# Sixteen bytes behind each half of a weight buffer: a Trainium2 decoder kernel whose weight tiles get six different start addresses modulo 128

## The chip, the cores and the metric

The kernel runs on one core of a Trainium2 chip. The time is device microseconds of one execution on that core. Engines are named as in the profile: PE is TensorE's matmul, PEld its weight load (of which each matmul has one of its own), DVE VectorE, ACT ScalarE, POOL GpSimd, and SP the engine that issues most DMAs.

## The reference, cut to what matters

Two decoder layers over 512 tokens of width 1024, in float32. Each layer has a half-step SwiGLU, a token mixer (retention in the first layer, forgetting attention in the second), a second half-step SwiGLU and a gated per-layer input ("PLE").

```
def swiglu(x, w_in, w_out):
    g, u = jnp.split(x @ w_in, 2, axis=-1)
    return (jax.nn.silu(g) * u) @ w_out

for i in range(2):
    h = h + 0.5 * swiglu(rmsnorm(h, nw[0]), ffn_w_in[i, 0], ffn_w_out[i, 0])
    h = h + (retention if i == 0 else forgetting_attention)(rmsnorm(h, nw[1]), ...)
    h = h + 0.5 * swiglu(rmsnorm(h, nw[2]), ffn_w_in[i, 1], ffn_w_out[i, 1])
    gate = sigmoid(rmsnorm(h, nw[3]) @ ple_w_gate[i])
    h = h + gate * (p[i] @ ple_w_proj[i])
return rmsnorm(h, final_norm_w)
```

d_model is 1024, d_ff 2816. All weights together are some 200 MB.

## The kernel before

Activations lie transposed: feature blocks of 128 partitions, tokens along the free axis. Each float32 operand is split into a high part, rounded to the fp32r format, and a low part (the rest, in fp32r too), and a product is three matmuls: high weight by high activation, high by low, low by high. `mm3` (L312 to L314) does this for the projections, mostly over 512 tokens at once, with the weight as the stationary operand. `v_part` (L678 to L680) has the weight as the moving operand. The input half of each SwiGLU uses a seven-product scheme on 256-token halves: `product` (L493) does twelve matmuls of 256 columns, four pairs with the high half of a weight tile and then four with the low half. Of the seven products of one block of w_in, two have the stored weights as stationary operand (tile `w`, read in `one` and `three`) and five have sums of weights (tiles `s`) or the remaining quarter (tile `a`); that is 24 matmuls of 84 with `w`. The first two blocks of each SwiGLU are done without the scheme by `plain` (L524), with `w` tiles and again 256 columns.

A weight tile goes through `Weights`. `load` (L75) issues a DMA into a raw buffer on SP. `split` (L82, L83) has ACT write the high half and DVE or POOL the low half. `negated` (L120 to L122) has ACT write the high half and the negated raw weight, and a DMA on POOL's queue adds the weight from memory onto the latter, which leaves the negative of the low half. Either way the tile `w` is one row of 2 x 1024 floats on each partition: the high half, then the low half 4096 bytes behind it.

PE's instructions stand in the order in which the code is written (`manual_schedule`); weights are fetched two tiles ahead of their use (`LOOKAHEAD = 2`, three wide buffers taken in turn). In the last PLE stage, which works on two halves of 256 tokens so that its weights are used twice, five of its wide tiles come from a pool `wkept` of their own.

Pools lie behind each other in SBUF in the order in which they are opened: const, hpool, ua, ub, uc, ud, wraw, wpool, tmp, stat, and behind these the pool of the stage that runs. The start addresses of the built program, in bytes from the start of a partition and modulo 128, are:

| tiles | before: start | start mod 128 of each half |
|---|---|---|
| unit_a, unit_b, unit_c, unit_d (activations), tmp, wraw, hall | 17952 to 177696 | 32 |
| `w`, the three wide buffers of wpool | 140832, 149024, 157216 | 32 and 32 |
| `s` and `a` of the SwiGLU pools | 192224 to 220896 | 96 and 96 |
| `w`, the five kept buffers of the last PLE stage | 184032 to 216800 | 96 and 96 |

A slice of 128 weights is 512 bytes and half of the tokens is 1024 bytes, so every operand slice of PE starts at its tile's value modulo 128.

Of the kernel before, what the change touches and what calls it, by code (L numbers as in the profile page):

```python
# [11 lines left out]
F32 = mybir.dt.float32  # L12
F32R = mybir.dt.float32r
# [4 lines left out]
P = 128  # L18
# [36 lines left out]
class Weights:  # L55
# [17 lines left out]
    def load(self, src):  # L73
        raw = self.raw_pool.tile([P, 1024], F32, name="wraw")
        self.nc.sync.dma_start(out=raw[:, : src.shape[1]], in_=src)  # L75
        return raw

    def split(self, raw, hi, lo, src=None):
        if self.low is None and src is not None:
            self.negated(raw, hi, lo, src)  # L80
            return
        self.nc.scalar.copy(hi, raw)  # L82
        self.low.tensor_tensor(out=lo, in0=raw, in1=hi.bitcast(F32), op=ALU.subtract)  # L83

    def chunk(self, src):
        n = src.shape[1]
        raw = self.load(src)
        if self.spare:
            tiles = [self.spare.pop(0)() for _ in range(4)]
            for i in range(2):  # L90
                self.split(raw[:, 512 * i : 512 * (i + 1)], tiles[i], tiles[2 + i])
            return Halves(tiles[0:2]), Halves(tiles[2:4])
        t = self.pool.tile([P, 2, 1024], F32R, name="w8")
        self.split(raw[:, :n], t[:, 0, :n], t[:, 1, :n], src)
        return t[:, 0, :], t[:, 1, :]

    def emit_parts(self, parts):

        nc = self.nc
        halves = lambda ap: ap.rearrange("p (h c) -> p h c", h=2)  # L100
        tiles = [
            (
                self.raw_pool.tile([P, 1024], F32, name="wraw"),
                self.pool.tile([P, 2, 1024], F32R, name="w8"),
            )
            for _ in range(2)
        ]
        for j0, j1 in parts:
            cs = slice(j0 * P, j1 * P)
            for src, (raw, t) in zip(self.plan, tiles):  # L110
                r, hi, lo = (halves(x)[:, :, cs] for x in (raw, t[:, 0, :], t[:, 1, :]))
                nc.sync.dma_start(out=r, in_=halves(src)[:, :, cs])
                nc.vector.tensor_copy(hi, r)
                nc.vector.tensor_tensor(out=lo, in0=r, in1=hi.bitcast(F32), op=ALU.subtract)
            yield
        self.ready += [(t[:, 0, :], t[:, 1, :]) for _, t in tiles]
# [7 lines left out]
    def first(self, pair):  # L124

        pair.raw = self.load(pair.q)
        pair.t = self.pool.tile([P, 2, 1024], F32R, name="w8")
        hi, lo = pair.t[:, 0, :], pair.t[:, 1, :]
        if pair.direct:
            self.split(pair.raw, hi, lo)  # L130
        else:
            self.negated(pair.raw, hi, lo, pair.q)
# [55 lines left out]
def trunk(ctx, tc, a):  # L188
    nc = tc.nc
# [6 lines left out]
    uc = ctx.enter_context(tc.tile_pool(name="uc", bufs=4))  # L196
    ud = ctx.enter_context(tc.tile_pool(name="ud", bufs=16))
    wraw = ctx.enter_context(tc.tile_pool(name="wraw", bufs=4))
    wpool = ctx.enter_context(tc.tile_pool(name="wpool", bufs=LOOKAHEAD + 1))
    tmp = ctx.enter_context(tc.tile_pool(name="tmp", bufs=7))  # L200
    stat = ctx.enter_context(tc.tile_pool(name="stat", bufs=1))
# [109 lines left out]
    def mm3(out, wh, wl, xh, xl, first, last):  # L311
        nc.tensor.matmul(out, wh, xh, start=first, stop=False)  # L312
        nc.tensor.matmul(out, wh, xl, start=False, stop=False)  # L313
        nc.tensor.matmul(out, wl, xh, start=False, stop=last)  # L314

    def halved(acc):
        hi, lo = temp(F32R), temp(F32R)
        split(acc, hi, lo)
        return hi, lo
# [13 lines left out]
    class Norm:  # L333
# [9 lines left out]
        def halves(self, b):  # L343
            if self.forms is not None:
                return self.quarters(b)
            hi, lo = self.unit(), self.unit()
            split(h[b], hi, lo, self.gain[:, b : b + 1])
            self.hi.append(hi)
            self.lo.append(lo)

        def plain(self, b):

            g = self.gain[:, b : b + 1]
            if b % 2:
                hi, lo = self.unit(), self.unit()
                split(h[b], hi, lo, g)
                both = [(hi[:, c], lo[:, c]) for c in HALVES]
            else:
                both = []
                for i, c in enumerate(HALVES):  # L360
                    u = self.unit() if i == 0 else unit(ud)
                    both.append(tuple(u[:, d] for d in HALVES))
                    split(h[b][:, c], *both[i], g)
            n = 1 + b % 2
            if n == 1:
                self.forms.append({})
            self.forms[b // 2].update({f"b{n}1": both[0], f"b{n}2": both[1]})
# [824 lines left out]
    norms[2].extra = ud  # L1192
    first = W.emit_parts(((0, 1), (1, 2), (2, 4)))
    next(first)
    load_x(1, 2)
    load_x(2, 4)
# [132 lines left out]
```

## Time and profile before

| | |
|---|---|
| time, median of 3 runs | 2228.97 us (2226.98 to 2231.87) |
| span of the profiled execution | 2230.5 us |
| PE busy | 2154.5 us, 97% of the span |
| PEld busy | 1937.5 us |
| DVE, ACT, POOL busy | 1447.1, 1212.3, 450.7 us |
| matmuls | 13525 |
| mean granted TensorE clock | 0.987 |
| DMA | 272 MB, 122 GB/s on the mean |

The profiled execution's own time is not listed apart from its span. The span is above the two faster of the three times, so if it is one of the three, it is the 2231.87 us one, with 1.4 us around the span.

How to read it: a row of the timeline gives start, length, engine, line and operation, `out<-in` by tile names, and the number of instructions merged. The length of a matmul is modelled from start to the end of its pipeline, and successive matmuls overlap; the distance between the starts of successive matmuls, here called the spacing, is what PE's time is made of. For a merged row the spacing is the distance to the start of the next row divided by the count.

### The profile page before, as it was taken

Reading aid. Unit: us, or ns where it says so; the run is one execution under the profiler, and the core shown is the slowest. Engines: PE = TensorE matmul, PEld = TensorE weight load, DVE = VectorE, ACT = ScalarE, POOL = GpSimd, SP = SyncE. Lnnn points to the kernel's source line nnn. Section 1 sums busy time; section 2 is a strip of 40 time slices with the busy share of each in tenths; the row PEclk is TensorE's granted clock in tenths of the full one; section 3 lists DMA queues with packets and bytes.
Section 4 is the critical chain, followed back from the end, with each engine's and each line's share of the span. In section 5 each row is a group of like instructions: output and inputs, shape, how many; then the busy total and the mean of one; then the engine's idle time right before and its main releaser. Section 6 shows DMA issues by size and latency. Waiting matters only on the chain.

```text
span 2230.5 us, 34455 instructions
## 1 busy us (share of the span) xinstructions
PE 2154.5 (97%) x13525; PEld 1937.5 (87%) x13525; DVE 1447.1 (65%) x2631; ACT 1212.3 (54%) x2037; POOL 450.7 (20%) x352
## 2 busy tenths in 40 slices
PE   7999999999999999999997999999999999999998
PEld 7999997888888798989876989898788888999987
DVE  8686776352542776767746677675675686777764
ACT  7565553433233663735555646364786775555543
POOL 0010003444444010101110001012334200110154
PEclk9999999999999999999998999999999999999999
DMA  5465563232222254746464457373622244655631
GB/s 176 113 163 150 138 161 95 81 99 76 88 83 76 85 137 119 170 133 152 129 151 117 114 136 182 113 167 103 153 91 87 69 116 112 159 158 137 152 104 39
DMA packets 86755, 272.33 MB, mean 122 GB/s; under 512 B 9520, under 2 KB 13104, under 8 KB 86592
## 3 DMA queue, kind: packets, MB, share of 16 engines
q1 hardware_dynamic: 63328, 209.78, 28.7%
q0 software_dynamic: 22032, 59.25, 15.9%
q8 instruction: 106, 1.74, 0.3%
q10 hardware_dynamic: 1232, 1.09, 0.1%
q14 instruction: 57, 0.47, 0.1%
HBM read 267.96 MB, written 2.13 MB: 121 GB/s over the span
## 4 chain that ended last, share of the span: by engine, by line
PE 80%; DVE 7%; ACT 6%; DMA 4%; issue 3%; POOL 0%; SPq 0%; DVEq 0%; ACTq 0%; POOLq 0%
PE bank L493 29%; PE bank L314 14%; PE bank L312 13%; PE bank L313 13%; PE bank L524 3%; DMA wraw<-in_ffn_w_in 3%; PE bank L678 2%; PE bank L679 2%; PE bank L680 2%; DVE w L83 1%; DMA w<-in_ple_gate 1%; DVE sums L151 1%; ACT p L982 1%; ACT w L82 1%; DVE tlo L303 1%
## 5 line engine op out<-in xcount | busy, mean ns | idle before, releaser
L82 ACT CAST w<-wraw 128x1024 fp32r<-128x1024 f32 (+1 forms) x232 | 235.1, 1021 | 431.0 <-PE bank L314 252.6
L314 PE MATMUL bank<-unit_a,w 128*128 128x512 f32 x736 | 288.9, 393 | 12.7 <-DMA w<-in_ple_gate 8.4
L312 PE MATMUL bank<-unit_a,w 128*128 128x512 f32 x736 | 289.8, 394 | 1.9 <-ACT w L82 1.6
L313 PE MATMUL bank<-unit_a,w 128*128 128x512 f32 x736 | 287.9, 391 | 0.2 <-DVE unit_a L303 0.2
L82 ACT CAST s<-sums 128x512 fp32r<-128x512 f32 x320 | 191.2, 617 | 155.3 <-DVE sums L151 106.6
L314 PE MATMUL bank<-unit_d,w 128*128 128x512 f32 (+1 forms) x712 | 268.1, 377 | 4.6 <-DVE w L83 4.6
L312 PE MATMUL bank<-unit_d,w 128*128 128x512 f32 (+1 forms) x712 | 269.2, 378 | 3.2 <-ACT w L82 1.6
L313 PE MATMUL bank<-unit_d,w 128*128 128x512 f32 (+1 forms) x712 | 268.3, 377 | 1.8 <-DVE unit_d L303 1.8
L83 DVE TENSOR_TENSOR s<-sums,s 128x512 fp32r<-128x512 f32 x320 | 213.7, 686 | 81.4 <-ACT s L82 80.4
L83 POOL TENSOR_TENSOR w<-wraw,w 128x1024 fp32r<-128x1024 f32 x83 | 202.6, 2445 | 233.5 <-ACT w L82 223.4
L122 POOL DMA_DIRECT2D a<-in_ffn_w_in x80 | 70.1, 876 | 651.4 <-ACT a L121 444.8
L83 DVE TENSOR_TENSOR w<-wraw,w 128x1024 fp32r<-128x1024 f32 (+1 forms) x149 | 175.8, 1185 | 28.3 <-ACT w L82 27.7
L493 PE MATMUL bank<-unit_b,s 128*128 128x256 f32 x880 | 185.9, 278 | 0.0
L493 PE MATMUL bank<-unit_d,s 128*128 128x256 f32 x1140 | 179.2, 277 | 0.0
L314 PEld LDWEIGHTS bank<-unit_a,w 128*128 128x128 f32 x736 | 138.8, 189 | 45.5 <-DMA w<-in_ple_gate 10.1
L493 PE MATMUL bank<-unit_a,s 128*128 128x256 f32 x1260 | 176.1, 277 | 1.9 <-ACT unit_a L376 1.1
L585 DVE SCALAR_TENSOR_TENSOR tmp<-bank,rows 128x512 f32<-128x512 f32 x96 | 66.0, 689 | 165.3 <-PE bank L314 164.0
L312 PEld LDWEIGHTS bank<-unit_a,w 128*128 128x128 f32 x736 | 139.0, 189 | 32.4 <-ACT w L82 3.5
L313 PEld LDWEIGHTS bank<-unit_a,w 128*128 128x128 f32 x736 | 139.0, 189 | 28.8 <-DVE unit_a L303 0.5
L493 PEld LDWEIGHTS bank<-unit_a,s 128*128 128x128 f32 x1260 | 158.8, 188 | 2.7 <-ACT unit_a L376 1.6
L314 PEld LDWEIGHTS bank<-unit_d,w 128*128 128x128 f32 x712 | 134.4, 189 | 30.5 <-DVE w L83 6.6
L312 PEld LDWEIGHTS bank<-unit_d,w 128*128 128x128 f32 x712 | 134.5, 189 | 30.3 <-ACT w L82 3.3
(270 smaller groups left out, 4801.1 us busy)
## 6 DMA issues: line engine op xcount, KB each, us to landing
wraw<-in_ffn_w_in SPq DMA_DIRECT2D x174, 512.0 KB, 4.3
wraw<-in_ffn_w_out SPq DMA_DIRECT2D x64, 512.0 KB, 4.7
w<-in_ffn_w_in POOLq DMA_DIRECT2D x58, 512.0 KB, 5.5
a<-in_ffn_w_in POOLq DMA_DIRECT2D x80, 256.0 KB, 6.2
wraw<-in_ffn_w_out SPq DMA_DIRECT2D x32, 384.0 KB, 3.7
wraw<-in_ret_qk SPq DMA_DIRECT2D x16, 512.0 KB, 3.5
wraw<-in_ret_v SPq DMA_DIRECT2D x16, 512.0 KB, 3.6
wraw<-in_ret_g SPq DMA_DIRECT2D x16, 512.0 KB, 3.5
```

What stands on the lines that cost most here:

```text
L82: self.nc.scalar.copy(hi, raw)
L83: self.low.tensor_tensor(out=lo, in0=raw, in1=hi.bitcast(F32), op=ALU.subtract)
L122: self.nc.gpsimd.dma_start(out=lo, in_=src, accum_op=ALU.add)
L312: nc.tensor.matmul(out, wh, xh, start=first, stop=False)
L313: nc.tensor.matmul(out, wh, xl, start=False, stop=False)
L314: nc.tensor.matmul(out, wl, xh, start=False, stop=last)
L493: add = lambda w, x, start, stop: nc.tensor.matmul(out, w, x, start=start, stop=stop, skip_group_check=True)
L524: nc.tensor.matmul(o[:, HALVES[t]], x[:, ks], y, start=k == t == q == 0, stop=k == KB - 1 and q == 2, skip_group_check=True,)
L585: nc.vector.scalar_tensor_tensor(out=t1, in0=o, scalar=-0.5, in1=n.r, op0=ALU.mult, op1=ALU.mult)
L678: nc.tensor.matmul(os[t], xh, wh[:, js], start=k == 0, stop=False)
L679: nc.tensor.matmul(os[t], xh, wl[:, js], start=False, stop=False)
L680: nc.tensor.matmul(os[t], xl, wh[:, js], start=False, stop=k == KB - 1)
```

## The change

Behind each half of a wide weight tile 16 bytes are left free, and a buffer of 32 bytes is put ahead of the pool, so that each half starts elsewhere modulo 128. The pools behind move by 32 + 3 x 32 = 128 bytes and keep their places modulo 128.

```diff
+    def wide(self):
+        return self.pool.tile([P, 2, 1028], F32R, name="w8")[:, :, 0:1024]
+
...
-        t = self.pool.tile([P, 2, 1024], F32R, name="w8")
+        t = self.wide()
...
-                self.pool.tile([P, 2, 1024], F32R, name="w8"),
+                self.wide(),
...
-        pair.t = self.pool.tile([P, 2, 1024], F32R, name="w8")
+        pair.t = self.wide()
...
     wraw = ctx.enter_context(tc.tile_pool(name="wraw", bufs=4))
+    nc.gpsimd.memset(ctx.enter_context(tc.tile_pool(name="gap0", bufs=1)).tile([P, 8], F32, name="gap0"), 0.0)
     wpool = ctx.enter_context(tc.tile_pool(name="wpool", bufs=LOOKAHEAD + 1))
```

| wide buffer, after | high half mod 128 | low half mod 128 |
|---|---|---|
| 140864 | 64 | 80 |
| 149088 | 96 | 112 |
| 157312 | 0 | 16 |
| the five kept ones | 96, 0, 32, 64, 96 | 112, 16, 48, 80, 112 |

No instruction moves: on every engine the order, the operand shapes and the waits are those of before, but for one added memset of 8 floats per partition, which stands as POOL's first instruction of the program body, ahead of the identity matrix.

## The prediction, made before the changed kernel ran

> **What bounds the kernel now.** I read the page first: the busy shares, then the chain that ended last.
>
> ```profile
> span 2230.5 us, 34455 instructions
> PE 2154.5 (97%) x13525; PEld 1937.5 (87%) x13525; DVE 1447.1 (65%) x2631; ACT 1212.3 (54%) x2037; POOL 450.7 (20%) x352
> PE 80%; DVE 7%; ACT 6%; DMA 4%; issue 3%; POOL 0%; SPq 0%; DVEq 0%; ACTq 0%; POOLq 0%
> ```
>
> PE carries 80% of the chain, and nothing else more than 7%. So the change is worth what it does to the spacing of matmuls. Next I read PE's timeline inside the first SwiGLU, where tiles `w`, `s` and `a` alternate while activations and columns stay alike.
>
> ```profile
> 302.13 1.60 PE L493 MATMUL bank<-unit_a,w 128*128 128x256 f32 x12
> 303.57 0.73 PE L493 MATMUL bank<-unit_b,s 128*128 128x256 f32 x5
> 304.13 0.50 PE L493 MATMUL bank<-unit_c,s 128*128 128x256 f32 x3
> 304.48 0.50 PE L493 MATMUL bank<-unit_b,s 128*128 128x256 f32 x3
> 304.81 0.28 PE L493 MATMUL bank<-unit_c,s 128*128 128x256 f32 x1
> 304.93 1.30 PE L493 MATMUL bank<-unit_a,s 128*128 128x256 f32 x10
> ```
>
> Twelve matmuls on `w` take 303.57 - 302.13 = 1.44 us, 120 ns each; twelve on `s` take 304.93 - 303.57 = 1.36 us, 113.3 ns each. Same form, same activations, 6.7 ns apart. The instructions of the line by tile, and one piece of the chain in order of time, say that this is the rule:
>
> ```profile
> L493 PEld LDWEIGHTS bank<-unit_a,s x1260: 186/188/330, 40.2 to 1081.3; 128*128 128x128 f32 x180
> L493 PEld LDWEIGHTS bank<-unit_a,w x540: 187/192/337, 55.9 to 1078.6; 128*128 128x128 f32 x180
> 127.02 77.44 PE bank L493 x672
> ```
>
> The median weight load is 192 ns from `w` and 188 ns from `s`, so the load is what lengthens. The piece holds eight blocks of 84: 8 x (24 x 120 + 60 x 113.3) = 77.4 us, the row exactly. By the address table, `w` starts at 32 modulo 128, as the activations do, and `s` and `a` at 96. Tile kind and address go together there; the last PLE stage separates them, where `w` tiles at 32 are followed by kept `w` tiles at 96, under the same line and activations.
>
> ```profile
> 2201.69 0.28 PE L312 MATMUL bank<-unit_c,w 128*128 128x256 f32 x1
> ...
> 2202.41 0.28 PE L312 MATMUL bank<-unit_d,w 128*128 128x256 f32 x1
> ...
> 2204.00 0.28 PE L314 MATMUL bank<-unit_d,w 128*128 128x256 f32 x1
> ...
> 2209.78 0.28 PE L312 MATMUL bank<-unit_d,w 128*128 128x256 f32 x1
> ...
> 2212.02 0.28 PE L313 MATMUL bank<-unit_d,w 128*128 128x256 f32 x1
> ```
>
> From 2201.69 to 2202.41, on tiles at 32, six spacings are 0.72 us: 120 ns. From 2202.41 to 2204.00, on a tile at 96, fourteen are 1.59 us: 113.6 ns. So the address matters, not the kind of tile. But from 2209.78 to 2212.02, on other kept tiles at 96, nineteen are 2.24 us: 117.9 ns. The address is not all; how the load falls against the running matmul matters too, and one pair of addresses can hold either spacing for long.
>
> **The change, part by part.** *Matmuls of 256 columns on `w`.* Their counts:
>
> ```profile
> L493 PE MATMUL bank<-unit_b,w 128*128 128x256 f32 x720 | 133.3, 285 | 11.4 <-ACT tmp L545 11.4
> L493 PE MATMUL bank<-unit_d,w 128*128 128x256 f32 x540 | 91.2, 286 | 0.0
> L493 PE MATMUL bank<-unit_a,w 128*128 128x256 f32 x540 | 82.1, 288 | 5.5 <-ACT tmp L545 5.5
> L493 PE MATMUL bank<-unit_c,w 128*128 128x256 f32 x120 | 27.8, 286 | 0.0
> L524 PE MATMUL bank<-unit_b,w x244: 276/283/580, 5.6 to 1825.6; 128*128 128x256 f32 x122
> L524 PE MATMUL bank<-unit_d,w x240: 278/283/415, 6.9 to 1829.9; 128*128 128x256 f32 x120
> L524 PE MATMUL bank<-unit_a,w x168: 279/283/283, 780.8 to 1829.2; 128*128 128x256 f32 x168
> L524 PE MATMUL bank<-unit_c,w x116: 279/283/384, 15.9 to 1827.0; 128*128 128x256 f32 x116
> ```
>
> L493 has 720 + 540 + 540 + 120 = 1920, L524 has 768; L524's median of 283 ns is that of L493's `w`, against 276 for `s`, so the same 120 ns is taken for it. All 2688 at 113.3 would save 2688 x 6.7 ns = 18.0 us: the upper end. The activations stay at 32. A third of the loads come from the buffer at 96 and 112, and two thirds of those from its high half: 597 loads at the pair (32, 96), which the trace shows at 113.3 in the SwiGLUs, 4.0 us. The other 2091 go to 64, 80, 112, 0 and 16, which no row shows; their gain lies between 13.9 us (as at 96) and nothing (as at 32), and below nothing too, since a load could become slower still: no row excludes it, and another 6.7 ns, the one step seen, would cost 13.9 us. The middle of the two spacings seen is nearest to the 117.9 ns row, so I take half, 7.0 us. Together -11.0 us. In PE's cover nothing stands in the way: in the stretch below, one SwiGLU with its norms, PE works 342 of 352 us and DVE, the next, 250.
>
> ```profile
> 43.00:395.00 352.00, 342.01 (x2303) 314.13 (x2304) 250.50 (x402) 186.31 (x303) 49.01 (x43) 0.99 0.51 135
> ```
>
> *Kept tiles of the last PLE stage.* Now at 96 with 113 to 118 ns; afterwards two of five high halves are at 96 again, one each at 0, 32 and 64. Some 200 matmuls by at most 6.7 ns either way: 1.3 us. I take nothing.
>
> *Matmuls of 512 columns.* These are the larger mass.
>
> ```profile
> L312 PE MATMUL bank<-unit_a,w 128*128 128x512 f32 x736 | 289.8, 394 | 1.9 <-ACT w L82 1.6 <-DVE tmp L1016 0.3
> L312 PE MATMUL bank<-unit_d,w 128*128 128x512 f32 x616 | 241.7, 392 | 3.2 <-ACT w L82 1.6 <-DVE unit_b L306 0.6 <-ACT unit_d L302 0.5
> 229.63 0.39 PE L314 MATMUL bank<-unit_d,w 128*128 128x512 f32 x1
> ...
> 231.90 0.39 PE L312 MATMUL bank<-unit_d,w 128*128 128x512 f32 x1
> 384.83 0.40 PE L314 MATMUL bank<-unit_a,w 128*128 128x512 f32 x1
> ...
> 386.91 0.39 PE L314 MATMUL bank<-unit_a,w 128*128 128x512 f32 x1
> ```
>
> From 229.63 to 231.90 ten spacings are 227 ns each, twice the 113.3. So at (32, 32) a long matmul already has its best spacing: the load has double the time, and its slowing is covered. This cover depends on the load ending early, which 4 to 7 ns cannot undo. I cost them at nothing. But between 384.83 and 386.91 nine spacings are 231.1 ns, in a stretch that had not settled. With three lines of 736 + 616, 4056 matmuls have `w` as stationary operand; if other addresses keep them unsettled, 4056 x 4.1 ns = 16.6 us are lost. A gain isn't excluded either: one step of 6.7 ns would be 27 us.
>
> *Writers of `w`.* ACT, DVE, POOL and the adding DMAs now write at other starts, the low halves at odd multiples of 16.
>
> ```profile
> w<-in_ffn_w_in POOLq DMA_DIRECT2D x58, 512.0 KB, 5.5
> w<-in_ple_gate POOLq DMA_DIRECT2D x7, 512.0 KB, 7.3
> PEld bank L314 <- DMA w<-in_ple_gate: 10.1, 4, 4.0
> PE bank L524 <- DMA w<-in_ffn_w_in: 9.3, 1, 9.3
> PEld bank L314 <- DVE w L83: 10.9, 9, 2.2
> L82 ACT CAST w<-wraw 128x1024 fp32r<-128x1024 f32 x200 | 208.7, 1050 | 360.0 <-PE bank L314 181.6 <-issue 96.1 <-PE bank L680 29.3
> L82 ACT CAST s<-sums 128x512 fp32r<-128x512 f32 x320 | 191.2, 617 | 155.3 <-DVE sums L151 106.6 <-PE bank L493 47.8
> ```
>
> Casting into `w` at 32 takes 1050 ns for 1024 elements, into `s` at 96 617 ns for 512: (1050 - 617) / 512 = 0.85 ns per element with 184 ns fixed, no trace of the address. PE waits for these writers 30 us in all in the three waits above; if starts at 16 made each writer a tenth slower, 3 us would be lost there; if faster, 3 us won. I take +1. The added memset of 8 floats stands ahead of 24 us in which POOL has nothing urgent: nothing. If its cover were gone, it would cost less than the 0.9 us of a DMA issue on that engine.
>
> **Sum.** -11.0 + 1 = -10 us against the profiled execution's 2230.5 us span, so 2220.5; against the median of 2229.0 the same -10 gives 2219.
>
> [...] The rows say 113.3 ns beside 120 ns under one line, and the faster when only the tile's address differs. [...]
>
> **The rivals.** *Nothing comes of it:* the other five starts hold 117.9 to 120 ns, only the 4.0 us at (32, 96) come, and writers or the kept tiles take it back: 2225 to 2233. For it: the kept tiles at 96 ran at 117.9 most of the time, and after each change of tile the load must find its place anew. Against: `s` and `a`, five sevenths of the SwiGLU's matmuls, hold 113.3 throughout. *The long matmuls lose their spacing:* with six starts instead of one, each change of tile, and of half, shifts the load against the matmul, and the 512-column matmuls run at 231.1 instead of 227 ns. The place is the output halves of the SwiGLUs, the mixers' projections and the gates. At the full price +16.6 - 10 = +6.6, 2236; without the gain on short ones 2246. It decides once 10 / 0.0041 = 2440 of the 4056 are unsettled. For it: 384.83 to 386.91. Against: at the pair (32, 96) short matmuls hold 113.3, half of 227. *The long ones gain a step too:* 2229 - 10 - 27 = 2192; nothing in the trace shows a spacing so short for long.
>
> **How the numbers follow.** Short matmuls gain and long ones stay: 0.50, own range 2211 (all 18 us) to 2224.5. Nothing: 0.24, 2224.5 to 2233.5. Long ones lose: 0.21, 2233.5 to 2246. Long ones gain: 0.05, below 2211. Two tenths of a per cent, 4.5 us, is about what a measurement of this kernel can tell from no change. Faster is 0.50 + 0.05 = 0.55, same 0.24, slower 0.21. The range 2208 to 2240 leaves out most of the last case and the dearer half of the third.
>
> **What would show it.** Right: the median load from `w` under `product` falls from 192 towards 188 ns, the stretch of 672 matmuls takes less than 77.4 us (76.2 if all gain), and rows of 512 columns stay 227 ns apart. Wrong: `w` rows still 120 apart; 512-column rows at 230 or more over whole stages; or the three waits for writers of `w` grow past 35 us. The prediction falls if spacing follows how the load is started rather than where it reads.

## The result, and the profile after

The changed kernel takes 2248.11 us (median of four runs, 2247.68 to 2248.78) against 2228.15 us for the kernel before (2226.98 to 2231.87): a ratio of 1.0083, with an interval of 1.0067 to 1.0099. The medians stand 20.0 us apart, a quotient of 1.0090, which lies inside that interval. A time of 2219 us and a range up to 2240 were forecast. The profiled execution took 2248.34 us with a span of 2246.5 us, 16.0 us more than the span before. Of all executions behind this document one, of the kernel pad256 below, took 2825.91 us at a granted clock of 0.713, and it is left out of every figure. Line numbers after are three or four higher: `product` is L497, `mm3` L316 to L318, `plain` L528.

The page's span, its busy shares and the chain that ended last:

```profile
span 2246.5 us, 34456 instructions
PE 2174.4 (97%) x13525; PEld 1937.3 (86%) x13525; DVE 1448.5 (64%) x2631; ACT 1213.6 (54%) x2037; POOL 451.1 (20%) x353
PE 83%; DVE 6%; ACT 5%; DMA 3%; issue 2%; POOL 0%; SPq 0%; DVEq 0%; ACTq 0%; POOLq 0%
```

Only PE's row grew by much, 19.9 us; the other engines are within 1.5 us of before, and PE now has 83% of the chain instead of 80%. So the time went into matmuls. Which ones, the timeline of PE says. The longest run of 512-column matmuls in which nothing waits has 244 of them, 243 spacings, from the last part of the first SwiGLU's output into the mixer. Its first and last row, in the kernel before:

```profile
322.85 0.40 PE L312 MATMUL bank<-unit_d,w 128*128 128x512 f32 x1
...
377.95 0.49 PE L312 MATMUL bank<-unit_a,w 128*128 128x512 f32 x1
```

and in the kernel after:

```profile
324.64 0.40 PE L316 MATMUL bank<-unit_d,w 128*128 128x512 f32 x1
...
380.98 0.46 PE L316 MATMUL bank<-unit_a,w 128*128 128x512 f32 x1
```

Before, 55.10 us, 226.7 ns a spacing; after, 56.34 us, 231.9 ns. This stretch, read the same way in every kernel below, is the measure of the long matmuls. The group of the line that showed 289.8 us and a mean of 394 ns before tells the same for the whole program:

```profile
L316 PE MATMUL bank<-unit_a,w 128*128 128x512 f32 x736 | 294.1, 400 | 1.8 <-ACT w L85 1.5
```

The short matmuls, by the chain's pieces in order of time (start, length, what):

```profile
126.57 77.87 PE bank L497 x672
...
1928.82 77.99 PE bank L497 x672
```

The piece of 672 was 77.44 us before and is not shorter but longer. Two places of PE's timeline inside a SwiGLU show why:

```profile
150.12 1.59 PE L497 MATMUL bank<-unit_a,w 128*128 128x256 f32 x12
151.55 0.73 PE L497 MATMUL bank<-unit_b,s 128*128 128x256 f32 x5
...
321.81 1.58 PE L497 MATMUL bank<-unit_a,s 128*128 128x256 f32 x12
323.22 0.75 PE L497 MATMUL bank<-unit_b,a 128*128 128x256 f32 x5
```

Twelve matmuls on `w` still take 1.43 us here, 119 ns each, and twelve on `s`, 113.3 ns each before, take 1.41 us, 117.5 ns each. The sums' buffers kept their starts modulo 128, but here their matmuls run at the slower of the two spacings that the forecast had seen on the kept tiles, 113.6 and 117.9 ns.

To see the whole, I took the distance from each row of PE's timeline to the next and put it to the form of the earlier one; distances over 270 ns (512 columns) or 135 ns (256 columns) for each matmul, and those up to a row that waited, are the rest.

| PE's time, us (count, mean) | before | after | difference |
|---|---|---|---|
| 512 columns | 1056.7 (4652, 227.2 ns) | 1079.6 (4656, 231.9 ns) | +22.9 |
| 256 columns on `w` | 344.5 (2871, 120.0 ns) | 339.4 (2866, 118.4 ns) | -5.1 |
| 256 columns on `s` and `a` | 533.4 (4702, 113.4 ns) | 542.0 (4713, 115.0 ns) | +8.6 |
| rest: waits, a lower clock, other forms | 286.2 | 275.8 | -10.4 |
| first to last matmul | 2220.8 | 2236.8 | +16.0 |

The long matmuls lost 22.9 us; the short ones won 5.1 us on `w` and lost more, 8.6 us, on `s` and `a`. In the rest, PE's waits for ACT's `tmp` in `product` fell from 16.9 to 12.5 us, and the mean granted clock of this execution was 0.989 against 0.987, an estimated 4 us (0.013 of the span before, less 0.011 of the span after); neither was tried by itself. The span of 2230.5 us before belongs to an execution about as long as the slowest of the four timed, so 16 us between the two traces and 20 us between the medians are no contradiction.

### The profile page after: what moved, and what is told of

Same layout as the page of the kernel before. It is cut to its first block, busy times and chain, and to the rows that moved or that the text cites. A ratio compares the mean times of both kernels' runs of the same rounds, so it can differ in the third digit from the quotient of the medians.

```text
span 2246.5 us, 34456 instructions
## 1 busy us (share of the span) xinstructions
PE 2174.4 (97%) x13525; PEld 1937.3 (86%) x13525; DVE 1448.5 (64%) x2631; ACT 1213.6 (54%) x2037; POOL 451.1 (20%) x353
## 4 chain that ended last, share of the span: by engine, by line
PE 83%; DVE 6%; ACT 5%; DMA 3%; issue 2%; POOL 0%; SPq 0%; DVEq 0%; ACTq 0%; POOLq 0%
PE bank L497 32%; PE bank L318 14%; PE bank L316 14%; PE bank L317 14%; PE bank L528 3%; PE bank L683 2%; PE bank L682 2%; PE bank L684 2%; DMA wraw<-in_ffn_w_in 1%; DMA w<-in_ple_gate 1%; DVE w L86 1%; ACT p L986 1%; ACT w L85 1%; ACT p L988 1%; DVE tlo L307 1%
## 5 line engine op out<-in xcount | busy, mean ns | idle before, releaser
L318 PE MATMUL bank<-unit_a,w 128*128 128x512 f32 x736 | 292.3, 397 | 12.9 <-DMA w<-in_ple_gate 8.5
L316 PE MATMUL bank<-unit_a,w 128*128 128x512 f32 x736 | 294.1, 400 | 1.8 <-ACT w L85 1.5
L317 PE MATMUL bank<-unit_a,w 128*128 128x512 f32 x736 | 291.1, 396 | 0.2 <-DVE unit_a L307 0.2
L316 PE MATMUL bank<-unit_d,w 128*128 128x512 f32 (+1 forms) x712 | 271.7, 382 | 3.3 <-ACT w L85 1.5
L318 PE MATMUL bank<-unit_d,w 128*128 128x512 f32 (+1 forms) x712 | 269.8, 379 | 4.7 <-DVE w L86 4.7
L497 PE MATMUL bank<-unit_b,s 128*128 128x256 f32 x880 | 187.9, 280 | 0.0
L318 PEld LDWEIGHTS bank<-unit_a,w 128*128 128x128 f32 x736 | 139.5, 190 | 49.4 <-DMA w<-in_ple_gate 9.9
L497 PE MATMUL bank<-unit_d,s 128*128 128x256 f32 x1140 | 181.1, 279 | 0.0
L497 PE MATMUL bank<-unit_a,s 128*128 128x256 f32 x1260 | 177.3, 278 | 1.9 <-ACT unit_a L380 1.1
L316 PEld LDWEIGHTS bank<-unit_a,w 128*128 128x128 f32 x736 | 139.3, 189 | 35.3 <-ACT w L85 3.5
L318 PEld LDWEIGHTS bank<-unit_d,w 128*128 128x128 f32 x712 | 133.9, 188 | 34.0 <-DVE w L86 6.6
L497 PEld LDWEIGHTS bank<-unit_a,s 128*128 128x128 f32 x1260 | 159.7, 188 | 2.7 <-ACT unit_a L380 1.6
L316 PEld LDWEIGHTS bank<-unit_d,w 128*128 128x128 f32 x712 | 133.5, 188 | 32.4 <-ACT w L85 3.3
```

What stands on the lines that cost most here:

```text
L497: add = lambda w, x, start, stop: nc.tensor.matmul(out, w, x, start=start, stop=stop, skip_group_check=True)
```

## The experiments

All starts below are differences: start of the weight tile minus start of the activations, modulo 256; that 256 is the period came out only on the way (long matmuls are 232.4 ns apart with 128 bytes more, in plus128, and 226.8 with multiples of 256 more, in pad256). The tables ahead of the prediction are modulo 128. By them `s` and `a` stand 64 bytes from the activations before and after; modulo 256 they stand at 192 before and at 64 after, since the pools behind moved by 128 bytes. A number such as 96, 48 or 224 in a kernel's name is a start with the activations at 32, so that it means a difference of 64, 16 or 192. The diffs are against the changed kernel where nothing else is said; `...` marks lines left out. In all of these kernels the five kept buffers of the last PLE stage have no padding; the two lines that see to this, in which `first_pool` is the pool of the three wide buffers, are shown once, in all96.

Each ratio is against runs of the kernel before that were timed together with it: their median is 2231.57 us for the first four experiments, 2229.39 us for the next four and 2230.55 us for the last three.

| kernel | long on `w` (three buffers) | short on `w` | `s`, `a` | 244-row stretch, us (ns a spacing) | ratio, interval |
|---|---|---|---|---|---|
| before | 0 | 0 | 192 | 55.10 (226.7) | 1 |
| after | 32+48, 64+80, 96+112 | the same | 64 | 56.34 (231.9) | 1.0083, 1.0067 to 1.0099 |
| all96 | 64 | 64 | 64 | 56.69 (233.3) | 1.0105, 1.0087 to 1.0124 |
| halves_differ | 0+16, 128+144, 0+16 | the same | 64 | 56.29 (231.6) | 1.0077, 1.0057 to 1.0097 |
| buffers_differ | 32, 64, 96 | the same | 64 | 56.68 (233.3) | 1.0105, 1.0084 to 1.0127 |
| all48 | 16, 144, 16 | the same | 64 | 56.70 (233.3) | 1.0085, 1.0065 to 1.0105 |
| plus128 | 128 | 128 | 64 | 56.47 (232.4) | 1.0088, 1.0058 to 1.0119 |
| both96 | 0 | 0 | 192 | 55.11 (226.8) | 0.9994, 0.9977 to 1.0010 |
| short96 | 0, 128, 0 | 64, 192, 64 | 64 | 55.94 (230.2) | 0.9997, 0.9981 to 1.0013 |
| long96 | 64, 192, 64 | 0, 128, 0 | 64 | 56.49 (232.5) | 1.0126, 1.0101 to 1.0151 |
| short96_256 | 0 | 64 | 192 | 55.11 (226.8) | 0.9959, 0.9941 to 0.9976 |
| short224_256 | 0 | 192 | 192 | 55.14 (226.9) | 1.0045, 1.0031 to 1.0059 |
| pad256 | 0 | 0 | 192 | 55.11 (226.8) | 1.0006, 0.9992 to 1.0020 |

Where one cell has two numbers they are the high and the low half.

### What of the six addresses does the harm?

Three theories. U: the starts are not uniform, so the load must find its place anew at each change of tile or half; one start for all would do no harm wherever it lies. P: the place itself, apart from that of the activations. M: the odd multiples of 16 at which the low halves begin.

**all96: one start for all, 64 bytes on.**

```diff
-        return self.pool.tile([P, 2, 1028], F32R, name="w8")[:, :, 0:1024]
+        if self.pool is not self.first_pool:
+            return self.pool.tile([P, 2, 1024], F32R, name="w8")
+        t = self.pool.tile([P, 2048], F32R, name="w8")[:, 0 : 2048]
+        return t.rearrange("p (a c) -> p a c", a=2)[:, :, 0:1024]
...
-    nc.gpsimd.memset(ctx.enter_context(tc.tile_pool(name="gap0", bufs=1)).tile([P, 8], F32, name="gap0"), 0.0)
+    nc.gpsimd.memset(ctx.enter_context(tc.tile_pool(name="gap0", bufs=1)).tile([P, 16], F32, name="gap0"), 0.0)
     wpool = ctx.enter_context(tc.tile_pool(name="wpool", bufs=LOOKAHEAD + 1))
+    nc.gpsimd.memset(ctx.enter_context(tc.tile_pool(name="gap1", bufs=1)).tile([P, 16], F32, name="gap1"), 0.0)
```

> Wide weight pool moved by 64 bytes, nothing between the halves, and a second gap of 64 bytes behind it, so that every weight half starts at 96 modulo 128 and all that lies behind keeps its place. Theory U (uniformity: the spacing of matmuls settles only where successive weight loads start at the same value modulo 128, and the changed kernel alternates): 512-column matmuls at 227 ns as before, 256-column ones on w tiles at 113 instead of 120, about 2228 - 17 = 2211 us. Theory P (place: each start has a spacing of its own against activations at 32, and 32 was the best for the long ones): 512-column matmuls at about 230.6 ns as the loads at 96 show in the changed kernel, +15 us on them and -17 on the short ones, 2222 to 2232 us. Theory M (odd multiples of 16 are what is slow): as U.

Measured 2253.53 us, 1.0105: no better than the change. The stretch of 244, in PE's timeline:

```profile
324.57 0.39 PE L320 MATMUL bank<-unit_d,w 128*128 128x512 f32 x1
...
381.26 0.45 PE L320 MATMUL bank<-unit_a,w 128*128 128x512 f32 x1
```

56.69 us, 233.3 ns a spacing, and steadily so: with one start for all buffers and halves, and an even one, the long matmuls are worse than with six. U and M fall. P survives only in kind: it had 230.6 ns and 2222 to 2232 us here, and the loss is larger. The same kernel shows something else in its chain:

```profile
126.99 79.15 PE bank L501 x672
...
894.48 76.17 PE bank L501 x672
```

Here `w`, `s` and `a` all stand at 64, so all 672 matmuls are alike in their starts; in the first SwiGLU they take 117.8 ns each, in the second 113.3. One pair of addresses holds either spacing, for a whole stage.

**halves_differ: 16 bytes behind the high half only, buffers 8320 bytes apart.**

```diff
-        return self.pool.tile([P, 2, 1028], F32R, name="w8")[:, :, 0:1024]
...
+        t = self.pool.tile([P, 2080], F32R, name="w8")[:, 0 : 2056]
+        return t.rearrange("p (a c) -> p a c", a=2)[:, :, 0:1024]
...
-    nc.gpsimd.memset(ctx.enter_context(tc.tile_pool(name="gap0", bufs=1)).tile([P, 8], F32, name="gap0"), 0.0)
```

> 16 bytes between the halves, but buffers a multiple of 128 bytes apart: in all three buffers the high half starts at 32 and the low half at 48. U: successive loads alternate inside every group of three, the long matmuls don't settle, 231 to 234 ns, 2243 to 2250 us. P: high halves at 32 keep 227 ns, only loads at 48 may be worse, 2229 to 2238 us. M: a third of the loads start at an odd multiple of 16, about all of the changed kernel's loss, 2243 to 2250 us.

Measured 2247.21 us, 1.0077, stretch 56.29 us. Two of three high halves are at 0 here, and every low half, which is one load of three, is elsewhere: that was enough to bring the mean of all long matmuls to 231.5 ns. The time lies where U and M had it, which had fallen already, and above the 2238 us that P allowed.

**buffers_differ: 32 bytes behind each tile, both halves alike.**

```diff
-        return self.pool.tile([P, 2, 1028], F32R, name="w8")[:, :, 0:1024]
...
+        t = self.pool.tile([P, 2056], F32R, name="w8")[:, 0 : 2048]
+        return t.rearrange("p (a c) -> p a c", a=2)[:, :, 0:1024]
```

> 32 bytes behind each whole tile, nothing between the halves: both halves of a buffer start alike, at 64, 96 and 0. U: matmuls settle inside a tile (24 or more on one tile) and are unsettled only behind a change of tile, long ones 227 to 229 ns on the mean, short ones on w 113 to 120, 2218 to 2237 us. P: long ones at 0 and 64 near 234.6 and at 96 near 229.6 ns as the changed kernel has for high after high, 2245 to 2252 us. M: no start is odd, 2211 to 2229 us.

Measured 2252.82 us, 1.0105, stretch 56.68 us: three different starts, all of them multiples of 32, cost what one start at 64 costs. U and M, which had 2237 us at most here, miss again, and P's 2252 us is passed by a little.

**all48: every half at an odd multiple of 16.**

```diff
-        return self.pool.tile([P, 2, 1028], F32R, name="w8")[:, :, 0:1024]
...
+        t = self.pool.tile([P, 2080], F32R, name="w8")[:, 4 : 2052]
+        return t.rearrange("p (a c) -> p a c", a=2)[:, :, 0:1024]
...
-    nc.gpsimd.memset(ctx.enter_context(tc.tile_pool(name="gap0", bufs=1)).tile([P, 8], F32, name="gap0"), 0.0)
```

> Every weight half in every wide buffer starts at 48 modulo 128, an odd multiple of 16, all uniform. U: long matmuls settle at 227 ns, short ones on w at 113 to 120, 2211 to 2230 us. P: unknown place, anything from 2211 to 2255 us. M: all loads are odd, slower than the changed kernel, over 2248 us.

Measured 2249.05 us, 1.0085. Two stretches of PE's timeline, 140 spacings of the first SwiGLU's output and the 243 of the measure:

```profile
218.19 0.39 PE L318 MATMUL bank<-unit_d,w 128*128 128x512 f32 x1
...
249.93 0.39 PE L320 MATMUL bank<-unit_d,w 128*128 128x512 f32 x1
...
324.27 0.40 PE L318 MATMUL bank<-unit_d,w 128*128 128x512 f32 x1
...
380.97 0.44 PE L318 MATMUL bank<-unit_a,w 128*128 128x512 f32 x1
```

31.74 us for 140 are 226.7 ns; 56.70 us for 243 are 233.3 ns. So long matmuls, too, have two states away from 0, a step of 6.6 ns apart, and odd multiples of 16 can hold the good one, for as long as a stage's part lasts. The time alone, over 2248 us, would have fitted M; these 140 spacings do not. What was left was that only the kernel before, with every long matmul on `w` at 0, had held it throughout.

### Does the place count, or the difference, and with which period?

E: the starts of weights and activations must be equal modulo 128. E256: modulo 256 or 512. P: 32 as such is the good place. A: what counts is that stretches with unlike starts follow each other.

**plus128: only a gap of 128 bytes ahead of the pool.**

```diff
-        return self.pool.tile([P, 2, 1028], F32R, name="w8")[:, :, 0:1024]
...
+        t = self.pool.tile([P, 2048], F32R, name="w8")[:, 0 : 2048]
+        return t.rearrange("p (a c) -> p a c", a=2)[:, :, 0:1024]
...
-    nc.gpsimd.memset(ctx.enter_context(tc.tile_pool(name="gap0", bufs=1)).tile([P, 8], F32, name="gap0"), 0.0)
+    nc.gpsimd.memset(ctx.enter_context(tc.tile_pool(name="gap0", bufs=1)).tile([P, 32], F32, name="gap0"), 0.0)
```

> Wide pool and all behind it moved by 128 bytes, no padding: every start modulo 128 is that of before, but weights no longer start at the activations' value modulo 256 or more. Theory E (a long matmul settles at 227 ns only where the next weights start at the activations' address modulo 128): 227 ns, time as before within 0.2%. Theory E256 (the period is 256 or 512): long matmuls 231 to 234 ns, slower by 15 to 25 us. Theory P (start 32 itself is the good place): as before.

Measured 2247.71 us, 1.0088. The measure in PE's timeline, and the chain's piece:

```profile
321.95 0.39 PE L319 MATMUL bank<-unit_d,w 128*128 128x512 f32 x1
...
378.42 0.45 PE L319 MATMUL bank<-unit_a,w 128*128 128x512 f32 x1
```

```profile
125.66 77.13 PE bank L500 x672
```

56.47 us, 232.4 ns: modulo 128 nothing has changed against the kernel before, and the loss is there in full. E falls, and with it the reading of addresses on which the forecast stood.

**both96: the same 64 bytes as in all96, but ahead of the activations, so that all moves together.** Against the kernel before:

```diff
+    nc.gpsimd.memset(ctx.enter_context(tc.tile_pool(name="gap0", bufs=1)).tile([P, 16], F32, name="gap0"), 0.0)
     hpool = ctx.enter_context(tc.tile_pool(name="hpool", bufs=1))
```

> A gap of 64 bytes ahead of the residual stream's pool, so that activations and wide weight tiles all start at 96 and the SwiGLU sums at 32: every difference is that of before, every place is another. E: time as before within 0.3%, 512-column matmuls 227 ns, 256-column ones on w 120. P: as the kernel with weights alone at 96, 231 to 234 ns and 15 to 25 us slower.

Measured 2228.20 us, 0.9994. The measure, and the chain's piece:

```profile
321.38 0.40 PE L313 MATMUL bank<-unit_d,w 128*128 128x512 f32 x1
...
376.49 0.49 PE L313 MATMUL bank<-unit_a,w 128*128 128x512 f32 x1
```

```profile
124.90 77.44 PE bank L494 x672
```

55.11 and 77.44 us, as before. The weights read from the same addresses as in all96, to the byte (140896, 149088, 157280), and lose nothing. So this place does no harm by itself; what the two kernels differ in is the distance to the activations. P falls.

**short96 and long96: the two kinds of `w` apart.** In short96 the tiles of SwiGLU inputs lie 64 bytes on within a buffer, the others at its start; in long96 it is the other way round. Buffers are 8320 bytes apart in both, which is 128 modulo 256. The diff of short96 is against the kernel before; in long96 the line with `at` reads `at = 0 if short else 16`:

```diff
+    def wide(self, short=False):
...
+        at = 16 if short else 0
+        t = self.pool.tile([P, 2080], F32R, name="w8")[:, at : at + 2048]
+        return t.rearrange("p (a c) -> p a c", a=2)
...
-        t = self.pool.tile([P, 2, 1024], F32R, name="w8")
+        t = self.wide(id(src) in self.short)
...
-                self.pool.tile([P, 2, 1024], F32R, name="w8"),
+                self.wide(True),
...
-        pair.t = self.pool.tile([P, 2, 1024], F32R, name="w8")
+        pair.t = self.wide(True)
...
+            W.short |= {id(pair.q), id(pair.r)}
```

> Buffers 8320 bytes apart; a tile of the SwiGLUs' input weights, which only 256-column matmuls read, starts 64 bytes into its buffer (96 modulo 128), any other tile at 32. E: long matmuls keep 227 ns, the 256-column ones on w go from 119.8 to about 114.6 ns as with all weights at 96, and those on sums rise by about 1 ns: 2688 x 5.2 ns = -14 us and +5 us, 2217 to 2222 us. Rival A (alternation of buffers between 32 and 96 is enough to unsettle the long ones): 231 ns or more on 512 columns, 2235 us or more.

> The reverse: tiles of the SwiGLUs' input weights at 32, all other wide tiles at 96. E: 512-column matmuls at about 233 ns, +28 us on 4650 of them, 256-column ones on w as before at 120: 2250 to 2260 us. If instead the loss of the kernel with all weights at 96 came from the sums or the writers, it would be less than 2240 us.

short96 took 2229.08 us, 0.9997, and long96 2257.75 us, 1.0126. The measure, in short96 and then in long96:

```profile
319.18 0.39 PE L321 MATMUL bank<-unit_d,w 128*128 128x512 f32 x1
...
375.12 0.46 PE L321 MATMUL bank<-unit_a,w 128*128 128x512 f32 x1
```

```profile
327.96 0.40 PE L321 MATMUL bank<-unit_d,w 128*128 128x512 f32 x1
...
384.45 0.44 PE L321 MATMUL bank<-unit_a,w 128*128 128x512 f32 x1
```

In long96 the stretch takes 56.49 us, in short96 55.94, between the two levels. There the buffers alternate: grouped by the buffer that each load reads, the long matmuls of short96 are 227.7 ns apart on the two buffers at 0 and 232.7 ns on the one at 128. So the loss follows the long matmuls' own starts, and E256 stands. E's time for short96, 2217 to 2222 us, is missed, since it takes all three buffers for equal; its time for long96, 2250 to 2260 us, is met. Not all of long96's loss is the long matmuls': by the sum over the timeline they cost 24.1 us against before, and the matmuls on `s` and `a` another 16.4 us, at 116.6 ns. A cannot be the cause by itself, since both kernels alternate in the same way and stand 28.7 us apart. The short ones of short96 on `w` fell to 114.6 ns, by the same sum 17.4 us, of which the long ones on the third buffer took back 7.6 us; the rest of that execution was 11.2 us longer, at a mean granted clock of 0.985. The next kernel takes what the third buffer spoilt.

### A version without the loss, and what padding costs by itself

**short96_256: as short96, buffers 8448 bytes apart**, so that every buffer's start is 0 modulo 256 for long matmuls and 64 for short ones, and the pools behind stay as they were modulo 256. Against short96:

```diff
-        t = self.pool.tile([P, 2080], F32R, name="w8")[:, at : at + 2048]
+        t = self.pool.tile([P, 2112], F32R, name="w8")[:, at : at + 2048]
```

> As the kernel with the SwiGLUs' input weights at 96 and all other wide tiles at 32, but buffers 8448 bytes apart, so that the long matmuls' weights start at the activations' address modulo 256 in all three buffers and not only in two. Theory E256 (a long matmul settles at 227 ns where weights and activations start alike modulo 256; short ones get 113 to 115 ns at 64 or 192): 512 columns at 227.2 ns in all buffers, 256 columns on w at 114, sums near 113.7: 2688 x 5.6 = -15 us, +1 for the sums, 2213 to 2217 us. Rival A (any tile at another start among the buffers unsettles the long ones): 229 ns or more, 2225 us or more.

Measured 2221.87 us (median of 11) against 2230.55 us, 0.9959, with an interval of 0.9941 to 0.9976: faster than both kernels, though 5 us above the 2213 to 2217 us that were expected. The page, the measure in the timeline, and the chain's piece:

```profile
span 2215.5 us, 34455 instructions
PE 2140.1 (97%) x13525; PEld 1922.7 (87%) x13525; DVE 1446.9 (65%) x2631; ACT 1211.8 (55%) x2037; POOL 449.5 (20%) x352
```

```profile
320.88 0.40 PE L321 MATMUL bank<-unit_d,w 128*128 128x512 f32 x1
...
375.99 0.49 PE L321 MATMUL bank<-unit_a,w 128*128 128x512 f32 x1
```

```profile
125.56 76.32 PE bank L502 x672
```

The long matmuls are back at 226.8 ns, and the piece is 76.32 us: all its 672 at 113.6 ns, which is what the forecast had hoped for. By the sum over the timeline, 256-column matmuls on `w` take 331.1 us against 344.5 before, 13.4 us less, of 15.0 us in the span. The profiled execution, at 2217.23 us, is among the shorter of the eleven, which lie from 2214.36 to 2231.96 us at granted clocks of 0.989 to 0.985; the medians are 8.7 us apart.

**short224_256: short ones at 192, where `s` and `a` stand already.** The last PLE stage's short tiles that come from the wide pool are put there as well. Against short96_256:

```diff
-        at = 16 if short else 0
+        at = 48 if short else 0
...
+        if l:
+            W.short |= {id(x) for x in ple_p[l] + ple_g[l]}
```

> The same with the short matmuls' weights 192 bytes into the buffer instead of 64, so that they start, against the activations, as the sums do (192 modulo 256), and with the last PLE stage's weights among them. E256: 512 columns at 227.2 ns, 256 columns on w 113.5 to 115, 1 us less than with 64 for the PLE stage: 2212 to 2217 us. If the state of the short ones depends on the step between w and sums, it differs from the 64 byte version by up to 6 us.

Measured 2242.35 us, 1.0045: a miss of both cases (2212 to 2217 us, or up to 6 us from short96_256), though no difference is new here. The long ones keep their 55.14 us. The chain's pieces:

```profile
125.96 79.14 PE bank L504 x672
...
1916.36 79.14 PE bank L504 x672
```

79.14 us are 117.8 ns for each of 672, `s` and `a` included, which hold 113.3 ns in the kernel before from the same place. At 192, short matmuls have two states: with `w` at 0 between them the sums stay in the fast one; with everything at 192 they stay in the slow one in all SwiGLUs. What follows what seems to matter, but it does not decide alone: in all96 one and the same order, all at 64, took 79.15 us in one SwiGLU and 76.17 in the next.

**pad256: the change with 256 bytes wherever it has 16 or 32.** Behind each half 256 bytes are free and the pool moves by 256, so that no start changes modulo 256:

```diff
-        return self.pool.tile([P, 2, 1028], F32R, name="w8")[:, :, 0:1024]
...
+        t = self.pool.tile([P, 2176], F32R, name="w8")[:, 0 : 2176]
+        return t.rearrange("p (a c) -> p a c", a=2)[:, :, 0:1024]
...
-    nc.gpsimd.memset(ctx.enter_context(tc.tile_pool(name="gap0", bufs=1)).tile([P, 8], F32, name="gap0"), 0.0)
+    nc.gpsimd.memset(ctx.enter_context(tc.tile_pool(name="gap0", bufs=1)).tile([P, 64], F32, name="gap0"), 0.0)
```

> The change with 256 bytes for each of its 16 and for its 32: as much padding in the same places, but all starts those of before modulo 256. E256: no change, 227 and 120 ns, 2229 us within 0.3%. If padding, moved pools or the writers cost anything by themselves, slower: 2233 to 2248 us.

Measured 2230.59 us (median of nine) against 2230.55, 1.0006: no difference. The measure, and the chain's piece:

```profile
321.56 0.40 PE L319 MATMUL bank<-unit_d,w 128*128 128x512 f32 x1
...
376.67 0.49 PE L319 MATMUL bank<-unit_a,w 128*128 128x512 f32 x1
```

```profile
125.53 77.44 PE bank L500 x672
```

Both are those of before. The padding, the moved pools, the memset and the strided writes and DMAs into two separate halves cost nothing that shows within the interval of 0.9992 to 1.0020, some 4 us upward; the change's 20 us come of the starts modulo 256. A period of 512 is not needed: the buffers of pad256 and of short96_256 stand at 0 and at 256 modulo 512 from the activations, and the long matmuls are 227.1 ns apart at either.

## Why the prediction was wrong, point by point

**The step that failed** is the one on matmuls of 512 columns: "This cover depends on the load ending early, which 4 to 7 ns cannot undo. I cost them at nothing." The cover was taken to hide a longer load. But the loads did not become longer. The instructions of the line by tile (shortest, median and longest in ns), before and after:

```profile
L314 PEld LDWEIGHTS bank<-unit_a,w x736: 186/188/334, 366.6 to 2153.0; 128*128 128x128 f32 x184
```

```profile
L318 PEld LDWEIGHTS bank<-unit_a,w x736: 186/188/330, 369.4 to 2170.9; 128*128 128x128 f32 x184
```

The median is 188 ns in both, and the spacing grew all the same, by 4.7 ns on the mean and by 6.6 ns where it is steady (all96, all48). That is the size of the step between 113.3 and 120 ns. A longer load is not in the trace, and that doubled time would have covered one was the author's estimate and was not shown. A stall that comes once for each matmul, at 256 columns as at 512, would fit; it is a guess, and no row of any run shows it.

**The rival that came true**, long matmuls that lose their spacing, was priced at +16.6 us: 4056 times 4.1 ns. Measured are +22.9 us: 4.7 ns, and some 4650 spacings, since the 576 matmuls of `v_part`, where the weight is the moving operand, lose as well (227.0 ns before, 231.8 after) and were not counted. Its size and direction came true, its reason did not: it blamed the changes between six starts, and all96, with one start for all, loses more (233.3 ns). What was said against it, that "at the pair (32, 96) short matmuls hold 113.3, half of 227", does not carry over: in all96, at that pair modulo 128, the short ones take 113.3 to 113.6 ns in three of the four pieces of 672, and the long ones 233.3.

**Short matmuls on `w`**, the -11.0 us of the sum, brought -5.1 us; all96, where each of them stands at 64, and short96_256 show how far the mean can fall, to 115 ns. The direction was right and the upper end near (13.4 of the 18.0 us come in short96_256); the share at other starts was guessed too high. The kept tiles, taken at nothing, are part of the -5.1 and were not measured apart.

**The matmuls on `s` and `a`** were not in the forecast's sum at all, and cost 8.6 us. The forecast saw two states at one address, 113.6 and 117.9 ns on the kept tiles, but took `s` and `a` to hold theirs "throughout"; short224_256 shows that from the same 192 they lose it once `w` stands there too. Their move from 192 to 64 is not enough for the loss: plus128 has them at 64 as well, and they hold 113.6 ns there.

**Addresses modulo 128** was the wrong modulus. Nothing in the trace of before could tell it: the differences there are 0 and 192 alone, and 0 and 64 modulo 128 part the tiles in the same way.

**Writers and the memset** were right in size: +1 us was taken, and the waits of PE for the writers were 30.3 us before and are 30.1 now, in the list of waits:

```profile
PEld bank L318 <- DMA w<-in_ple_gate: 9.9, 3, 4.0
PE bank L528 <- DMA w<-in_ffn_w_in: 9.1, 1, 9.1
PEld bank L318 <- DVE w L86: 11.1, 9, 2.2
```

**The signs that were named.** The median load from `w` was to fall from 192 to 188 ns if the forecast was right, and it did:

```profile
L497 PEld LDWEIGHTS bank<-unit_a,w x540: 186/188/333, 54.4 to 1084.9; 128*128 128x128 f32 x180
```

But the piece of 672, which was to follow it below 77.4 us, rose to 77.87. In short224_256 the median is 188 ns as well, at 117.8 ns a spacing. The length of a load is no witness of the spacing, and it was the evidence for "so the load is what lengthens". The other signs were good ones: rows of 512 columns at 230 or more over whole stages stand in the trace, as the wrong case named them.

**Both operands' starts** count, and together: plus128 has the wide weight tiles of before 128 bytes on, both96 has weights and activations moved alike, and their long matmuls are 232.4 and 226.8 ns apart over the measure. The forecast was right to take the address of the weights for a cause and wrong in thinking that this spoke for a gain.

**Open.** Which of two states a stretch falls into, away from equal starts, is not settled; that it is "how the load falls against the running matmul", as the forecast had it, was the author's estimate, and no run shows it. In all48 the eight stretches that hold 226.7 ns each begin behind a wait of PE of 0.64 to 0.71 us for DVE's half of `w`, and the measure, at 233.3, begins without one; but in all96 those behind the same wait hold 233.3 to 233.4, so the wait alone does not decide. It was not tried further.

## What to carry to other kernels

Before shifting or padding a buffer that PE reads, write down its start minus that of the other operand, modulo 256 at least, and keep the difference for every matmul whose spacing is already the best; here 0 for the 512-column matmuls was worth 23 us, and keeping it cost nothing that shows (pad256, 1.0006). A gain that one form of an instruction has from a new place must be shown for the other forms that read from there, and where they disagree they may be given different places in one buffer (0.9959). A duration in the trace, such as the median of the loads (188 ns under L314 and L318, with long matmuls 227.2 and 231.9 ns apart), is not the spacing: measure the change by start-to-start distances over a whole undisturbed stretch.

## What the hardware showed that was not expected

With float32r operands of 512 columns, the spacing was 226.7 to 226.9 ns over the stretch in all five kernels whose long matmuls have weights and activations that start equal modulo 256, and 230.2 to 233.3 ns in the eight others. With 256 columns it is the reverse: 120 ns at equal starts, and 113.3 or 117.8 ns at 64 and at 192, two states that last for whole stages at the same addresses. In the pair of kernels that tests it, the difference of the two starts counts and the place does not: the same weight addresses gave 233.3 ns with the activations 64 bytes before them modulo 256, and 226.8 ns with the activations moved along.
